# Moving the weight buffers of a split-precision transformer kernel to four different byte offsets from their matmul operands

## Chip, cores and metric

One Trainium2 chip, one NeuronCore of it. The metric is the device time of one execution of the whole program in microseconds (us), on that core. Engines are named as in the profile: PE is TensorE's matmul, PEld its weight load, DVE is VectorE, ACT is ScalarE, SP is the engine that issues the DMAs.

## What is computed

Two transformer blocks on 512 tokens of width 1024, all in float32. The first block has two layers; each is a SwiGLU feed-forward, a hybrid mixer (sliding-window attention, a gated linear recurrence, a short convolution) and a second feed-forward. The second block has one layer with low-rank attention, gated linear attention and a convolutional feed-forward. Cut to what the time goes into, it is a long row of products of the tokens with weights:

```python
def swiglu(h, w_gu, w_down):
    gu = h @ w_gu
    g, u = jnp.split(gu, 2, axis=-1)
    return (jax.nn.silu(g) * u) @ w_down
...
for l in range(DEPTH):
    h = modulate(x, g_norm[l, 0], mod[:, 0], mod[:, 1])
    x = x + 0.5 * mod[:, 2][:, None, :] * swiglu(h, w_ffn1_gu[l], w_ffn1_down[l])
    h = modulate(x, g_norm[l, 1], mod[:, 3], mod[:, 4])
    x = x + mod[:, 5][:, None, :] * hybrid_mixer(h, w_in[l], w_out[l], ...)
    h = modulate(x, g_norm[l, 2], mod[:, 6], mod[:, 7])
    x = x + 0.5 * mod[:, 8][:, None, :] * swiglu(h, w_ffn2_gu[l], w_ffn2_down[l])
```

## The kernel before

**Products in three matmuls.** [...] A product of weights w and tokens x is then made of three matmuls that add up in one PSUM bank: low weights with high tokens, high weights with low tokens, high weights with high tokens. The method `mm` issues them (lines 500, 501 and 502), eight chunks of 128 rows one after another, so 24 matmuls for one unit of weights with 128 output channels. In a matmul the weights are the stationary operand (`lhsT`, 128 columns, loaded by a LDWEIGHTS of its own before each matmul), the tokens are the moving one (`rhs`, 512 or 256 columns).

**Where the operands lie.** The token parts lie in slots of 2048 bytes in each partition: 36 slots `r0` to `r35`, and in most phases eight extra ones in the tile `xr` (method `xtype`). The weights come by DMA into a ring of four buffers `raw` (4096 bytes in each partition, 1024 float32). For each unit `split_next` takes the next buffer of the pool `hip` (tile `whi`) and of the pool `lop` (tile `wlo`); each pool has `WB` = 4 buffers, handed out in turn, so a unit belongs to one of four rounds. The method `split` fills both: ACT copies `raw` to `whi` (line 507), DVE writes `raw` minus `whi` to `wlo` (line 508). There are 450 such units, nearly all of 1024 or 896 columns.

**Addresses.** Pools are laid out one behind the other. In the program before, each slot `r` starts at 128 bytes past a multiple of 512 in its partition, and so does `xr`, because of a pool `gap` of 384 bytes that nothing uses. All eight weight buffers start at 384 past a multiple of 512 (`whi` from byte 173440, `wlo` from byte 189824, in steps of 4096). A matmul takes a piece of 128 columns, 512 bytes, from a weight buffer. So in every matmul of line 500, 501 or 502 the distance from the moving operand to the weights is 256 bytes, modulo 512.

**Order.** The order of instructions on each engine follows from the order in which the program issues them and from waits on tiles; addresses have no part in it. TensorE's weight load of the next matmul stands right behind the start of the current one.

Of the kernel before, what the change touches and what calls it, by code (L numbers as in the profile page):

```python
# [9 lines left out]
F32 = mybir.dt.float32  # L10
F32R = mybir.dt.float32r
# [16 lines left out]
P = 128  # L28
# [173 lines left out]
class Arena:  # L202


    def __init__(self):
        self.tiles = []
        self.free = []
        self.cur = 0
# [133 lines left out]
class Prog:  # L342
# [4 lines left out]
    def __init__(self, es, tc, d, out):  # L347
        self.es, self.tc, self.d, self.out = es, tc, d, out
        nc = self.nc = tc.nc
        self.T, self.V, self.A = nc.tensor, nc.vector, nc.scalar  # L350

        def mk(n, b, **k):
            return es.enter_context(tc.tile_pool(name=n, bufs=b, **k))

        cp = self.cp = mk("cp", 1)
        self.rawp = mk("rawp", self.RAW)
        self.hip = mk("hip", self.WB)
        self.lop = mk("lop", self.WB)
        self.sm = mk("sm", 12)
        mk("gap", 1).tile([P, 96], F32, name="gap")  # L360
        self.banks = Banks(tc)
        self.park = mk("dp", 1, space=bass.MemoryType.DRAM).tile([KD, P, S], F32, name="park")
        self.logits = mk("dl", 1, space=bass.MemoryType.DRAM).tile([16, P, S], F32, name="logits")
        self.F = Arena()
        self.F.add(cp.tile([P, self.NF * 512], F32, name="farena"), self.NF * 2)
        self.R = Slots([cp.tile([P, S], F32R, name=f"r{i}")[:, :] for i in range(36)])
        self.RX = Slots()
        self.xpool = None
        self.vecs = cp.tile([P, d["vecs"].shape[1]], F32, name="vecs")
        self.cst = cp.tile([P, 3 * P], F32, name="cst")  # L370
        self.ident = self.cst[:, 0:P]
        self.maskf, self.maskb = self.cst[:, P:2 * P], self.cst[:, 2 * P:3 * P]
        self.ones = cp.tile([P, P], F32, name="ones")
        self.eps = cp.tile([P, 1], F32, name="eps")
        self.sinks = cp.tile([P, 16], F32, name="sinks")
        self.nsink = cp.tile([P, 16], F32, name="nsink")
        self.mod = [cp.tile([P, 72], F32, name=f"mod{l}") for l in range(2)]
        self.mod2 = cp.tile([P, 48], F32, name="mod2")
        self.modc = cp.tile([P, 16], F32, name="modc")
        self.crow = [None] * 3  # L380
        self.units = []
        self.ready = {}
        self.ld = self.sp = self.tk = self.rt = self.nsplit = 0
        self.bg = []
        self.users, self.loader = [], None
# [69 lines left out]
    def split_next(self):  # L455
        u = self.units[self.sp]
        if self.ld <= self.sp:
            self.load_next()
        kind, ap, key, raw = u
        n = ap.shape[-1]  # L460
        if kind == "w":
            h = self.hip.tile([P, 1024], F32R, name="whi", tag="whi")
            lo = self.lop.tile([P, 1024], F32R, name="wlo", tag="wlo")
            self.split(raw[:, :n], h[:, :n], lo[:, :n])
            self.ready[self.nsplit] = (key, h, lo)
            self.nsplit += 1
        else:
            self.mod_unit(key, raw)
            if self.sp < EARLY:
                raw.done()  # L470
        u[3] = None
        self.sp += 1
        ahead = self.RAW + (4 if self.sp < EARLY - 8 else 0)
        while self.ld < len(self.units) and self.ld < self.sp + ahead:
            self.load_next()
# [1572 lines left out]
```

## Time and profile before

| | |
|---|---|
| median of 3 runs | 2715.85 us (2713.94 to 2716.39) |
| the profiled execution, its own time | 2715.99 us |
| its span, first to last instruction | 2714.2 us |
| PE busy | 2679.2 us, 99% |
| PEld busy | 2250.4 us, 83% |
| DVE busy | 1668.5 us, 61% |
| ACT busy | 1024.1 us, 38% |
| DMA queue q1 | 353.64 MB, 40.3% of 16 engines |
| granted TensorE clock, mean | 0.994 |

The span is the stretch of the profiled execution between its first and last instruction; the execution's own time is 1.8 us longer. A busy share is a mean over the whole span. [...]

### The profile page before, as it was taken

The numbers are of one execution on the slowest core, as the hardware profiler recorded it, in microseconds if no ns is written. First come the engines' busy times: TensorE is split into PE (matmuls) and PEld (weight loads), VectorE is DVE, ScalarE is ACT, GpSimd is POOL, SyncE is SP. The second block draws the span as 40 slices with busy tenths as digits, with TensorE's granted clock in tenths as the row PEclk, the third lists the DMA queues.
The fourth block names the chain that finished last, engine by engine and source line by source line (L and its number), as shares of the span: only waits on it lengthen the run. The fifth ranks groups of instructions, "written<-read, shape, count | busy, mean of one in ns | idle before, by whom it ended". The sixth has DMA issues, their size and how long they took to land.

```text
span 2714.2 us, 34099 instructions
## 1 busy us (share of the span) xinstructions
PE 2679.2 (99%) x13586; PEld 2250.4 (83%) x13586; DVE 1668.5 (61%) x2854; ACT 1024.1 (38%) x1603; POOL 0.2 (0%) x4
## 2 busy tenths in 40 slices
PE   8999999999999999999999999999999999999998
PEld 7888897898888988889879888888788767988887
DVE  7554468664444744446866865474576665786666
ACT  3322237442222422223654232253444664432322
POOL 0000000000000000000000000000000000000000
PEclk8999999999999999999999999999999999999999
DMA  7544443344444444444423666423222104233332
GB/s 286 194 140 149 152 141 131 115 142 146 147 151 146 139 158 145 149 144 155 146 71 113 209 208 195 147 88 117 82 91 70 58 28 155 86 101 97 91 98 64
DMA packets 105887, 355.81 MB, mean 131 GB/s; under 512 B 11776, under 2 KB 14976, under 8 KB 105472
## 3 DMA queue, kind: packets, MB, share of 16 engines
q1 hardware_dynamic: 105728, 353.64, 40.3%
q8 instruction: 106, 1.74, 0.3%
q14 instruction: 53, 0.43, 0.1%
HBM read 345.21 MB, written 8.39 MB: 130 GB/s over the span
## 4 chain that ended last, share of the span: by engine, by line
PE 93%; DVE 3%; ACT 2%; issue 1%; DMA 0%; SPq 0%; DVEq 0%; ACTq 0%
PE pb L500 28%; PE pb L501 28%; PE pb L502 28%; PE pb L1775 1%; PE pd L1747 1%; ACT farena L401 1%; PE pd L1764 1%; PE pb L618 1%; PE pb L2024 1%; PE pb L1168 1%; PE pb L2027 0%; PE pb L2028 0%; PE pb L1642 0%; PE pb L1115 0%; PE pb L1152 0%
## 5 line engine op out<-in xcount | busy, mean ns | idle before, releaser
L500 PE MATMUL pb<-r,wlo 128*128 128x512 f32 (+1 forms) x3360 | 1236.4, 369 | 1.2 <-DVE wlo L508 1.1
L501 PE MATMUL pb<-r,whi 128*128 128x512 f32 (+1 forms) x3360 | 1229.2, 367 | 0.0
L502 PE MATMUL pb<-r,whi 128*128 128x512 f32 (+1 forms) x3360 | 1229.1, 366 | 0.0
L507 ACT ACTIVATE whi<-raw 128x1024 fp32r<-128x1024 f32 (+2 forms) x450 | 465.0, 1034 | 807.5 <-issue 441.7
L500 PEld LDWEIGHTS pb<-r,wlo 128*128 128x128 f32 x3360 | 633.4, 189 | 113.3 <-issue 7.3
L502 PEld LDWEIGHTS pb<-r,whi 128*128 128x128 f32 x3360 | 634.1, 189 | 103.2 <-issue 0.2
L501 PEld LDWEIGHTS pb<-r,whi 128*128 128x128 f32 x3360 | 634.1, 189 | 102.3 <-issue 1.9
L508 DVE TENSOR_TENSOR wlo<-raw,whi 128x1024 fp32r<-128x1024 f32 (+2 forms) x450 | 535.9, 1191 | 207.9 <-ACT whi L507 207.0
L512 DVE CUSTOM_DVE_ANT_0 raw<-raw,farena 128x1024 f32<-128x1024 f32 x176 | 215.2, 1224 | 204.1 <-DMA raw<-wmod 144.3
L677 DVE SCALAR_TENSOR_TENSOR farena<-pb,mod,farena 128x512 f32<-128x512 f32 (+1 forms) x176 | 114.9, 653 | 203.8 <-PE pb L502 203.4
L500 PE MATMUL pb<-xr,wlo 128*128 128x512 f32 (+1 forms) x520 | 186.3, 358 | 0.0
L501 PE MATMUL pb<-xr,whi 128*128 128x512 f32 (+1 forms) x520 | 185.4, 356 | 0.0
L502 PE MATMUL pb<-xr,whi 128*128 128x512 f32 (+1 forms) x520 | 185.3, 356 | 0.0
L401 ACT ACTIVATE farena<-pb 128x512 f32<-128x512 f32 x93 | 55.6, 598 | 329.5 <-PE pb L502 325.5
L768 DVE TENSOR_TENSOR farena<-pb,farena 128x512 f32<-128x512 f32 x110 | 75.9, 691 | 158.9 <-PE pb L502 141.8
L820 DVE SCALAR_TENSOR_TENSOR farena<-pb,vecs,farena 128x441 f32<-128x441 f32 (+2 forms) x176 | 120.7, 693 | 42.7 <-ACT farena L812 39.4
L500 PEld LDWEIGHTS pb<-xr,wlo 128*128 128x128 f32 x520 | 98.2, 189 | 14.4 <-ACT xr L507 0.2
L501 PEld LDWEIGHTS pb<-xr,whi 128*128 128x128 f32 x520 | 98.3, 189 | 14.4 <-DVE xr L508 0.2
L502 PEld LDWEIGHTS pb<-xr,whi 128*128 128x128 f32 x520 | 98.2, 189 | 14.1
L574 ACT ACTIVATE farena<-farena 128x256 f32<-128x256 f32 (+1 forms) x97 | 44.9, 468 | 84.7 <-DVE farena L677 84.7
L401 ACT ACTIVATE farena<-farena 128x512 f32<-128x512 f32 (+2 forms) x89 | 51.3, 605 | 64.5 <-DVE farena L820 47.7
L645 ACT ACTIVATE r<-farena,mod 128x256 fp32r<-128x256 f32 (+1 forms) x119 | 55.4, 516 | 51.1 <-DVE farena L643 50.6
(275 smaller groups left out, 1843.9 us busy)
## 6 DMA issues: line engine op xcount, KB each, us to landing
raw<-gu SPq DMA_DIRECT2D x213, 512.0 KB, 3.6
raw<-wmod SPq DMA_DIRECT2D x128, 512.0 KB, 3.5
raw<-dn SPq DMA_DIRECT2D x80, 448.0 KB, 3.4
raw<-wada SPq DMA_DIRECT2D x48, 512.0 KB, 3.5
raw<-dn SPq DMA_DIRECT2D x40, 512.0 KB, 3.8
raw<-w2a SPq DMA_DIRECT2D x34, 512.0 KB, 3.5
raw<-win SPq DMA_DIRECT2D x32, 512.0 KB, 3.5
raw<-wout SPq DMA_DIRECT2D x24, 512.0 KB, 3.5
```

Of the source, the lines that this page charges most:

```text
L401: i = self.A.activation(out, in_, func, **k).ins
L500: self.T.matmul(acc, lhsT=lo[:, s], rhs=xh[:, tok], start=i == 0, stop=False)
L501: self.T.matmul(acc, lhsT=h[:, s], rhs=xl[:, tok], start=False, stop=False)
L502: self.T.matmul(acc, lhsT=h[:, s], rhs=xh[:, tok], start=False, stop=i == n - 1)
L507: self.A.activation(hi, src, AF.Copy)
L508: self.V.tensor_tensor(lo, src, hi.bitcast(F32), op=SUB)
L512: self.V.tensor_tensor_reduce(out=out, in0=raw, in1=row, scale=1.0, scalar=0.0, op0=MUL, op1=ADD, accum_out=col)
L574: self.A.activation(t[:, :n], src, AF.Square, scale=scale)
L645: self.A.activation(hi[:, tok], t[:, :n], AF.Identity, bias=sh[:, k:k + 1])
L677: self.V.scalar_tensor_tensor(x, acc[:, :n], gate[:, d:d + 1], x, op0=MUL, op1=ADD)
L768: self.V.tensor_tensor(a[:, :], acc[:, :], g[:, :], op=MUL)
L820: self.V.scalar_tensor_tensor(o, g[:, r0 + i - 1:r1 + i - 1, c0 + j - 1:c1 + j - 1], self.v(f"cw{i}{j}", f), o, op0=MUL, op1=ADD)
```

## The change

It adds two unused tiles of 256 bytes, cuts the one behind the small tiles from 384 to 128 bytes, and makes the weight buffers 1040 columns wide instead of 1024, of which the last 16 are never touched.

```diff
         self.rawp = mk("rawp", self.RAW)
+        mk("gap0", 1).tile([P, 64], F32, name="gap0")
         self.hip = mk("hip", self.WB)
+        mk("gap1", 1).tile([P, 64], F32, name="gap1")
         self.lop = mk("lop", self.WB)
         self.sm = mk("sm", 12)
-        mk("gap", 1).tile([P, 96], F32, name="gap")
+        mk("gap2", 1).tile([P, 32], F32, name="gap2")
...
-            h = self.hip.tile([P, 1024], F32R, name="whi", tag="whi")
-            lo = self.lop.tile([P, 1024], F32R, name="wlo", tag="wlo")
+            h = self.hip.tile([P, 1040], F32R, name="whi", tag="whi")
+            lo = self.lop.tile([P, 1040], F32R, name="wlo", tag="wlo")
```

A buffer is now 4160 bytes, 64 more than a multiple of 512, so the four rounds start at different places. What the built programs hold (bytes past a multiple of 512, in each partition; the distance is weights minus moving operand, modulo 512):

| | before | changed |
|---|---|---|
| slots r | 128 | 128 |
| whi and wlo, rounds 1 to 4 | 384, 384, 384, 384 | 128, 192, 256, 320 |
| extra slots xr | 128 | 384 |
| distance to r, rounds 1 to 4 | 256 in all | 0, 64, 128, 192 |
| distance to xr, rounds 1 to 4 | 256 in all | 256, 320, 384, 448 |

In a unit the high and the low part stand at the same distance. The order of instructions on every engine is the same in both programs, row for row, with the same waits; only line numbers and addresses differ.

## Rows read from the trace of the kernel before

**Rows 1.** The page, part 1: busy time and share of the span by engine

```profile
PE 2679.2 (99%) x13586; PEld 2250.4 (83%) x13586; DVE 1668.5 (61%) x2854; ACT 1024.1 (38%) x1603; POOL 0.2 (0%) x4
```

**Rows 2.** The page, part 4: the chain that ended last, by engine and by line

```profile
PE 93%; DVE 3%; ACT 2%; issue 1%; DMA 0%; SPq 0%; DVEq 0%; ACTq 0%
PE pb L500 28%; PE pb L501 28%; PE pb L502 28%; PE pb L1775 1%; PE pd L1747 1%; ACT farena L401 1%; PE pd L1764 1%; PE pb L618 1%; PE pb L2024 1%; PE pb L1168 1%; PE pb L2027 0%; PE pb L2028 0%; PE pb L1642 0%; PE pb L1115 0%; PE pb L1152 0%
```

**Rows 3.** The page, part 5, line 500 with slots r and xr: count, busy us, mean ns

```profile
L500 PE MATMUL pb<-r,wlo 128*128 128x512 f32 (+1 forms) x3360 | 1236.4, 369 | 1.2 <-DVE wlo L508 1.1
...
L500 PE MATMUL pb<-xr,wlo 128*128 128x512 f32 (+1 forms) x520 | 186.3, 358 | 0.0
```

**Rows 4.** Timeline of PE, 512 columns, feed-forward (start us, duration us, what): steps 0 and 24

```profile
1000.03 0.39 PE L502 MATMUL pb<-r,whi 128*128 128x512 f32 x1
...
1005.47 0.39 PE L502 MATMUL pb<-r,whi 128*128 128x512 f32 x1
```

**Rows 5.** Timeline of PEld, the weight load beside the matmul at 1000.03

```profile
1000.03 0.19 PEld L500 LDWEIGHTS pb<-r,wlo 128*128 128x128 f32 x1
```

**Rows 6.** Timeline of PE, 256 columns, slots r and xr mixed: steps 0 and 24

```profile
367.08 0.28 PE L501 MATMUL pb<-r,whi 128*128 128x256 f32 x1
...
369.96 0.28 PE L501 MATMUL pb<-r,whi 128*128 128x256 f32 x1
```

**Rows 7.** Timeline of PE at half clock: steps 0 and 3

```profile
450.61 0.63 PE L502 MATMUL pb<-r,whi 128*128 128x512 f32 x1
...
451.89 0.63 PE L502 MATMUL pb<-r,whi 128*128 128x512 f32 x1
```

**Rows 8.** Windows, full and half clock: stretch, busy by engine, PEclk, DMA share, GB/s

```profile
441.00:442.00 1.00, 1.00 (x6) 0.84 (x5) 0.97 (x2) 0.97 (x2) 0.00 (x0) 1.00 0.79 270
450.60:452.20 1.60, 1.60 (x5) 1.30 (x4) 1.59 (x9) 0.00 (x0) 0.00 (x0) 0.50 0.21 36
```

**Rows 9.** Timeline of PE, attention scores, distance 0: two pairs of 512 and 256 columns

```profile
2150.93 0.39 PE L1747 MATMUL pd<-xr,r 128*128 128x512 f32 x1
2151.16 0.28 PE L1748 MATMUL pd<-xr,r 128*128 128x256 f32 x1
...
2151.62 0.40 PE L1747 MATMUL pd<-xr,r 128*128 128x512 f32 x1
```

**Rows 10.** Timeline of PE after a stretch of other matmuls (line 1046): steps 0 to 3 and 8

```profile
428.20 0.40 PE L501 MATMUL pb<-r,whi 128*128 128x512 f32 x1
428.43 0.40 PE L502 MATMUL pb<-r,whi 128*128 128x512 f32 x1
428.66 0.40 PE L500 MATMUL pb<-r,wlo 128*128 128x512 f32 x1
428.90 0.39 PE L501 MATMUL pb<-r,whi 128*128 128x512 f32 x1
...
430.05 0.39 PE L500 MATMUL pb<-r,wlo 128*128 128x512 f32 x1
```

**Rows 11.** Lines by form, the two halves of the split: count, busy us, mean ns

```profile
L507 ACT ACTIVATE whi<-raw 128x1024 fp32r<-128x1024 f32 x356 | 376.7, 1059 | 604.4 <-issue 315.2 <-PE pb L502 260.5 <-PE pb L1433 20.3
L508 DVE TENSOR_TENSOR wlo<-raw,whi 128x1024 fp32r<-128x1024 f32 x356 | 434.8, 1222 | 172.7 <-ACT whi L507 171.9
```

**Rows 12.** The tile wlo: who waited for it (us, times)

```profile
  PEld pb L500: 1.3, 1
  PE pb L500: 1.1, 1
```

## The prediction

> **What bounds the kernel now.** I read the page from the top. The busy line says that PE works 99% of the span while DVE and ACT stand at 61% and 38% [rows 1]; the chain that ended last is PE for 93%, and 84% of it lies on the three lines 500, 501 and 502, in equal parts [rows 2]. So the time is the number of matmuls on these lines times the step from one start to the next, and the other engines matter only where PE waits for them. The count is 3360 with slots `r` and 520 with `xr` on line 500 [rows 3]; lines 501 and 502 have the same, which makes 3 x 3880 = 11640 matmuls. Some 400 more at the program's start and in the second block also use `whi` or `wlo`; I leave them out of the sum.
>
> The reader should not take the step from a matmul's duration, since matmuls overlap. In the timeline of a feed-forward 24 steps run from 1000.03 to 1005.47 us [rows 4], which is 5.44 us / 24 = 226.7 ns. [...] While a matmul runs, the weights of the next are being loaded; the load's row starts in the same hundredth of a microsecond [rows 4, 5]. [...]
>
> **The change part by part.** *Instructions.* None is added, removed or moved, on any engine or DMA queue, and the waits are the same. Cost 0.
>
> *The splits.* ACT and DVE still write 1024 columns for most units, at 1059 and 1222 ns [rows 11], to addresses that are shifted by multiples of 64 bytes. No row shows another offset, so I bound the effect by the cover: in the whole span PE waited 1.1 us, once, for `wlo`, and the weight load 1.3 us, once [rows 12], while DVE was idle for 39% of the span [rows 1]. A split slower by a tenth would add 0.12 us to each of 450 units, 55 us of DVE work beside some 1046 us that it has free; without that cover it would cost these 55 us. A faster one gives nothing. Cost 0.
>
> *The padding.* 64 unused bytes per buffer and three gaps; nothing reads them. Cost 0.
>
> *The distances.* This is the whole question. Before, all 11640 matmuls run at distance 256 modulo 512. Afterwards each round has a quarter of them, 2910: with slots `r` at 0, 64, 128 and 192, with `xr` at 256, 320, 384 and 448. The trace of before has no matmul at a distance of 64, 128 or 192, so its nearest rows must bound them:
>
> - Distance 0 is there: in the attention scores (lines 1747 and 1748) keys in `xr` stream past queries in `r`, both 128 bytes past a multiple of 512. Two pairs of 512 and 256 columns take 2151.62 - 2150.93 = 0.69 us, 345 ns a pair [rows 9]. At distance 256 such a pair is 226.7 + 120.0 = 346.7 ns [rows 4, 6]. That is the same within the 10 ns to which the rows are printed. So the round at 0 costs nothing.
> - Between buffers of one kind the addresses differ by multiples of 512, and `r` and `xr` lie in different parts of the memory. In the stretch of 256 columns both kinds alternate and the steps stay at 120.0 ns [rows 6]. So the upper address bits do nothing either.
> [...]
> - Upwards, the slowest step of such matmuls in these rows is 0.24 us, from 428.66 to 428.90 [rows 10], 13.3 ns over the settled one: 3 x 2910 x 13.3 ns = 116 us more.
>
> I take **0** for the three unseen distances, because the two that the trace does show, as far apart as the modulus 512 allows, agree, and so do `r` and `xr`. This is the nearest evidence, but it is evidence for two of eight places.
>
> [...]
>
> The sum: the profiled execution's own 2715.99 us + 0, which is 0.1 us off the median of the three runs, 2715.85 us. Forecast **2716 us**, with a range of its own of 2711 to 2721. Of this kernel a measurement can tell about 0.2%, 5.4 us, from no change.
>
> **The rivals.** *The rhythm is lost (slower).* The 226.7 ns are a rhythm into which the matmuls settle. After other work the steps wander: 8 steps from 428.20 to 430.05 us take 1.85 us, 231.3 ns each, with single steps of 230 and 240 ns [rows 10], before they settle. [...] The place is lines 500 to 502. If every unit, now at another distance than the one before, has to settle again, the price is 8 x (231.3 - 226.7) = 37 ns for 450 units: 17 us, 2733 us. If the steps never settle at the three new distances, it is 8730 x 4.6 ns = 40 us: **2756 us**. The bound is 2832 us, where each step takes 240 ns. [...] For it speaks the wandering itself; against it that distance 0 and distance 256, and a change from one to the other, cost the same.
>
> [...]
>
> *The change does not do what it says.* Then all rounds would stand at one distance. The addresses of the built program exclude this; and its time would be 2716 us too, so it gets no chance of its own.
>
> **How the numbers follow.** The forecast, no effect, gets 0.42: the seen distances agree, but six of eight are unseen. Slower gets 0.38: when a distance matters at all, mixing four of them in turn gives the rhythm three ways to be worse and a switch at each unit. Faster gets 0.20: it needs a freed round that is not given back by the others. These are also the chances of slower by over 0.2%, of within 0.2% and of faster by over 0.2%. For the range, the lower end is one freed round, 2677 us; more than one freed round, some 0.08, is left out. The upper end is half of the upper bound, 58 us: 2774 us, which holds both prices of the lost rhythm; the worse half, some 0.12, is left out.
>
> **What would show it.** In the timeline of the changed kernel the steps of lines 500 to 502 must be read unit by unit: in four units in a row, 24 steps each. All at 226.7 ns means that the forecast and its reason hold. [...] The pairs of lines 1747 and 1748, whose keys move from distance 0 to 256, should stay at 345 ns. The splits should stay near 1059 and 1222 ns, and PE's waits for `wlo` near 1 us. I am wrong if any round's step differs by over 1 ns from 226.7, since 2910 matmuls then already make 3 us; and wrong in the reasoning, though not in the time, if rounds differ and cancel.

## The result, and the profile after

The changed kernel takes 2742.62 us (median of four runs, 2740.77 to 2743.15). Beside it the kernel before took 2715.18 us (four runs, 2713.94 to 2716.39). The ratio is 1.010, with a 95% interval from 1.0082 to 1.0117: **slower by 1.0%**, inside the range of the prediction but not its forecast. The profiled execution took 2743.13 us with a span of 2741.4 us; the span before was 2714.2 us. Both have a mean granted clock of 0.994, so the 27.2 us between the spans are not the clock's.

The page of the changed kernel: busy time by engine, the chain by engine, and the groups that answer to [rows 3] (lines stand two lower, so 500 is now 502).

```profile
PE 2707.4 (99%) x13586; PEld 2247.0 (82%) x13586; DVE 1669.3 (61%) x2854; ACT 1022.4 (37%) x1603; POOL 0.2 (0%) x4
...
PE 93%; DVE 4%; ACT 2%; issue 1%; DMA 0%; SPq 0%; DVEq 0%; ACTq 0%
...
L502 PE MATMUL pb<-r,wlo 128*128 128x512 f32 (+1 forms) x3360 | 1245.0, 372 | 1.4 <-DVE wlo L510 1.2
...
L502 PE MATMUL pb<-xr,wlo 128*128 128x512 f32 (+1 forms) x520 | 187.0, 360 | 0.0
```

The counts are those of before, to the instruction. PE is busy 28.2 us longer (2707.4 against 2679.2) [rows 1], the others are as long as before to within 4 us. The chain is PE's for 93%, as it was [rows 2]. So the same matmuls are slower, and no new wait appears. Two views confirm the second half. The splits, by form, against [rows 11]:

```profile
L509 ACT ACTIVATE whi<-raw 128x1024 fp32r<-128x1024 f32 x356 | 376.1, 1057 | 625.8 <-issue 324.3 <-PE pb L504 273.1 <-PE pb L1435 20.7
...
L510 DVE TENSOR_TENSOR wlo<-raw,whi 128x1024 fp32r<-128x1024 f32 x356 | 434.5, 1221 | 192.7 <-ACT whi L509 192.2
```

And who waited for the tile `wlo`, against [rows 12]:

```profile
  PEld pb L502: 1.4, 1
  PE pb L502: 1.2, 1
```

Splits of 1057 and 1221 ns, and one wait of 1.2 us: nothing has changed here. What has changed is the step from one start to the next. The timeline of PE shows four units of a feed-forward in a row, at distances 128, 64, 0 and 192; of each unit the first and the last start of a run of steps stand here, of the second also the three behind the first.

```profile
1001.67 0.40 PE L503 MATMUL pb<-r,whi 128*128 128x512 f32 x1
...
1006.55 0.40 PE L503 MATMUL pb<-r,whi 128*128 128x512 f32 x1
...
1007.02 0.39 PE L502 MATMUL pb<-r,wlo 128*128 128x512 f32 x1
1007.25 0.40 PE L503 MATMUL pb<-r,whi 128*128 128x512 f32 x1
1007.49 0.39 PE L504 MATMUL pb<-r,whi 128*128 128x512 f32 x1
1007.72 0.40 PE L502 MATMUL pb<-r,wlo 128*128 128x512 f32 x1
...
1012.15 0.39 PE L503 MATMUL pb<-r,whi 128*128 128x512 f32 x1
...
1013.31 0.39 PE L502 MATMUL pb<-r,wlo 128*128 128x512 f32 x1
...
1018.07 0.39 PE L502 MATMUL pb<-r,wlo 128*128 128x512 f32 x1
1018.30 0.39 PE L503 MATMUL pb<-r,whi 128*128 128x512 f32 x1
1018.53 0.39 PE L504 MATMUL pb<-r,whi 128*128 128x512 f32 x1
...
1023.11 0.39 PE L503 MATMUL pb<-r,whi 128*128 128x512 f32 x1
```

- Distance 128: 21 steps in 4.88 us, 232.4 ns each.
- Distance 64: 22 steps in 5.13 us, 233.2 ns. Single steps alternate, 0.23 and 0.24 us.
- Distance 0: 21 steps in 4.76 us, 226.7 ns. This is the step of before [rows 4]. The stretch begins behind the unit's first three steps, which still take 229 to 232 ns.
- Distance 192: 20 steps from 1018.53, in 4.58 us, 229.0 ns.

The granted clock from 1000 to 1024 us is 1.00 in both kernels.

With 256 columns the same view shows the opposite. Here a unit at distances 0 and 256 ends, and one at 192 and 448 begins at 382.89:

```profile
380.73 0.28 PE L502 MATMUL pb<-r,wlo 128*128 128x256 f32 x1
...
382.89 0.28 PE L502 MATMUL pb<-xr,wlo 128*128 128x256 f32 x1
...
385.16 0.28 PE L504 MATMUL pb<-xr,whi 128*128 128x256 f32 x1
```

18 steps in 2.16 us are 120.0 ns, as in [rows 6]; the 20 steps that follow take 2.27 us, 113.5 ns. At half clock there is no such difference. Five steps at distance 128, and the window with its PEclk of 0.50:

```profile
456.56 0.63 PE L504 MATMUL pb<-r,whi 128*128 128x512 f32 x1
...
458.69 0.63 PE L503 MATMUL pb<-r,whi 128*128 128x512 f32 x1
```

```profile
456.60:458.60 2.00, 2.00 (x6) 1.61 (x5) 1.95 (x11) 0.00 (x0) 0.00 (x0) 0.50 0.29 96
```

2.13 us / 5 = 426 ns, as in [rows 7], whose clock is 0.50 as well [rows 8].

The score pairs of the attention, whose keys have moved from distance 0 to 256, against [rows 9]; the last row is the first matmul behind two pairs:

```profile
2176.76 0.39 PE L1749 MATMUL pd<-xr,r 128*128 128x512 f32 x1
...
2177.46 0.40 PE L503 MATMUL pb<-r,whi 128*128 128x512 f32 x1
```

Two pairs take 0.70 us, before 0.69.

**Where the 27 us are.** For each matmul with a weight piece as stationary operand the step up to its start can be read from the timeline and sorted by the distance that the built program gives it, here modulo 256. Means in ns; left out are steps over 153 ns for 256 columns or 287 ns for 512, which hold a wait or run at half clock, and the few short ones, up to 29 ns for 256 columns and 202 ns for 512 (together 2% of the steps, as many after as before):

| distance | before: 0 | after: 0 | 64 | 128 | 192 |
|---|---|---|---|---|---|
| 512 columns | 227.00 | 227.98 | 233.27 | 232.66 | 229.08 |
| such matmuls | 9084 | 2313 | 2271 | 2241 | 2259 |
| 256 columns | 119.83 | 119.64 | 115.73 | 118.54 | 116.34 |
| such matmuls | 2760 | 678 | 702 | 690 | 690 |

Number times difference: 2313 x 0.98 + 2271 x 6.27 + 2241 x 5.66 + 2259 x 2.08 ns = +33.9 us, and 678 x -0.19 + 702 x -4.10 + 690 x -1.29 + 690 x -3.49 ns = -6.3 us. Together +27.6 us, against 27.2 us between the spans: within the accuracy of such a sum the steps of these lines are the whole difference.

### The profile page after: what moved, and what is told of

Read it like the earlier page. It is cut to its first block, busy times and chain, and to the rows that moved or that the text cites. A ratio compares the mean times of both kernels' runs of the same rounds, so it can differ in the third digit from the quotient of the medians.

```text
span 2741.4 us, 34099 instructions
## 1 busy us (share of the span) xinstructions
PE 2707.4 (99%) x13586; PEld 2247.0 (82%) x13586; DVE 1669.3 (61%) x2854; ACT 1022.4 (37%) x1603; POOL 0.2 (0%) x4
## 4 chain that ended last, share of the span: by engine, by line
PE 93%; DVE 4%; ACT 2%; issue 1%; DMA 0%; SPq 0%; DVEq 0%; ACTq 0%
PE pb L502 28%; PE pb L503 28%; PE pb L504 28%; PE pb L1777 1%; ACT farena L403 1%; PE pd L1749 1%; PE pd L1766 1%; PE pb L620 1%; PE pb L1170 1%; DVE wlo L510 0%; PE pb L1644 0%; PE pb L1117 0%; PE pb L1154 0%; PE pb L1433 0%; PE pb L1435 0%
## 5 line engine op out<-in xcount | busy, mean ns | idle before, releaser
L510 DVE TENSOR_TENSOR wlo<-raw,whi 128x1024 fp32r<-128x1024 f32 (+2 forms) x450 | 535.4, 1190 | 230.7 <-ACT whi L509 230.0
L576 ACT ACTIVATE farena<-farena 128x256 f32<-128x256 f32 (+1 forms) x97 | 44.8, 467 | 83.6 <-DVE farena L679 83.6
```

Source lines behind the costliest of these rows:

```text
L510: self.V.tensor_tensor(lo, src, hi.bitcast(F32), op=SUB)
L576: self.A.activation(t[:, :n], src, AF.Square, scale=scale)
```

## Experiments

Each changes the kernel before, but for e8. In e1 to e7 and e9 the weight buffers are 1088 columns wide (4352 bytes), and the piece in use begins `o` columns in, so that `o` sets the distance in steps of 4 bytes:

```diff
-            h = self.hip.tile([P, 1024], F32R, name="whi", tag="whi")
-            lo = self.lop.tile([P, 1024], F32R, name="wlo", tag="wlo")
-            self.split(raw[:, :n], h[:, :n], lo[:, :n])
+            o = 0
+            h = self.hip.tile([P, 1088], F32R, name="whi", tag="whi")[:, o:o + n]
+            lo = self.lop.tile([P, 1088], F32R, name="wlo", tag="wlo")[:, o:o + n]
+            self.split(raw[:, :n], h, lo)
```

**One distance for all (e1, e2, e9).** e1 is this diff: wider buffers, rounds at 256 and 0 in turn. e2 has `o = 16` (distance 64), e9 has `o = 4` (distance 16), each modulo 256.

> Weight buffers 4352 bytes long instead of 4096, so that the four rounds stand at distances 256 and 0 modulo 512 in turn; no 64, 128 or 192. Theory A (the distance modulo 256 sets the step of a matmul, and 0 and 256 are the same place): 2715 us, as before, with 226.7 ns per 512 columns and 120 ns per 256. Rival B (changing the distance from unit to unit disturbs the rhythm, whatever the distances are): slower, up to the 2742 us of the change. Rival C (longer buffers or moved small tiles cost by themselves): 2742 us.

> As e1, but every unit is written 64 bytes into its buffer, so that all matmuls with weights run at distance 64 modulo 256 and none changes. Theory A: the steps that the changed kernel shows in its round at 64, 233.3 ns per 512 columns and 115.7 ns per 256, now in all: 9084 x 6.3 ns - 2760 x 4.1 ns = +57 - 11 us, 2761 us. Rival B (the mixing costs): no switches, so 2715 us.

> All units 16 bytes into their buffers, so every product runs at distance 16. In the scan by 16 bytes a unit at 16 came after one at 0 and took 227 to 228 ns per 512 columns; in the scan by 4 bytes it came after one at 12 and took 233 ns. If a distance has two rhythms and the matmuls before decide which is taken, this kernel shows both in turn, or one of them throughout: 9084 x 0 to 6.3 ns, 2713 to 2772 us. If the distance alone decides, all its steps are 227 to 228 ns and it takes 2715 to 2724 us.

Measured: e1 2715.14 us, ratio 1.0002 [0.9993, 1.0011], steps 227.02 and 119.82 ns. Padding, another pitch and a change between 256 and 0 at each unit cost nothing. e2 2758.04 us, 1.0164 [1.015, 1.0178], steps 233.34 and 115.18 ns: by the sum above 9084 x 6.34 - 2760 x 4.65 ns = +44.8 us, and 42.9 us came. So the cost comes with the distance itself, with no mixing of distances. e9 2763.94 us, 1.0178 [1.0163, 1.0193], the slowest of all, 233.02 and 118.37 ns. The timeline of PE of e2:

```profile
1000.27 0.40 PE L501 MATMUL pb<-r,wlo 128*128 128x512 f32 x1
...
1005.87 0.40 PE L501 MATMUL pb<-r,wlo 128*128 128x512 f32 x1
```

And of e9, two stretches:

```profile
441.06 0.39 PE L503 MATMUL pb<-r,whi 128*128 128x512 f32 x1
...
446.50 0.39 PE L503 MATMUL pb<-r,whi 128*128 128x512 f32 x1
...
1000.17 0.40 PE L502 MATMUL pb<-r,whi 128*128 128x512 f32 x1
...
1005.77 0.40 PE L502 MATMUL pb<-r,whi 128*128 128x512 f32 x1
```

At 1000 us each kernel has 24 steps in 5.60 us, 233.3 ns: these are not steps that wander for a while and settle, but a lasting pace. The stretch of e9 at 441 us has 24 steps in 5.44 us, 226.7 ns, at the same distance of 16 and at full clock (at half clock 24 steps would take 10.2 us, at 426 to 427 ns each). So this distance has two lasting rhythms, as the first of the two cases in the expectation had it.

The traces show when one is taken: where a stream of matmuls begins. Call a stream a row of matmuls of one width that no longer step interrupts. e9 has 17 streams of 512 columns with 35 steps or more. Behind their first few steps 13 of them run at 233 ns to their end, one over 1487 steps, and 4 at 227 ns; none changes on the way. In the kernel before, at distance 0, all 20 such streams come down to 227 ns within some ten steps and stay there. In e2, at distance 64, all 17 stay at 233 ns.

**Which operand's place (e10, e11, e8).** e10 moves slots and weights by 64 bytes together; e11 moves the slots by 64 bytes and leaves the weights where they were, both modulo 256; e8 is the changed kernel with the extra slots `xr` put back to the place that `r` has, modulo 512.

```diff
 e10 and e11, ahead of the slots:
+        cp.tile([P, 16], F32, name="pada")
 e11 also, behind them:
+        cp.tile([P, 48], F32, name="padb")
-        mk("gap", 1).tile([P, 96], F32, name="gap")
+        mk("gap", 1).tile([P, 112], F32, name="gap")
 e8, against the changed kernel:
-        mk("gap2", 1).tile([P, 32], F32, name="gap2")
+        mk("gap2", 1).tile([P, 96], F32, name="gap2")
```

> The kernel before with 64 unused bytes ahead of the slots: slots and weight buffers all move by 64, the distance stays 256. Theory A (the distance between the two counts): 2715 us, 226.7 ns per 512 columns. Rival E (the place of the weights by themselves counts: 128 bytes past a multiple of 256 is the good one, now it is 192): the steps that the change shows one place further on, 233.3 ns, 2758 us.

> The kernel before with the slots r and xr moved by 64 bytes and the weight buffers by 256: the weights stay at 128 past a multiple of 256, the distance becomes 192 modulo 256. Theory A: the changed kernel's steps at 192 in all matmuls, 9084 x 2.2 ns - 2760 x 3.9 ns = +20 - 11 us, 2724 us. Rival E: 2715 us.

> The change with one part undone: the unused tile behind the small tiles is 384 bytes again, so that the extra slots xr stand like the slots r and all products run at 0, 64, 128 and 192 in turn. Theory A (distance modulo 256): the 256 bytes do nothing, 2742 us as with the change. Rival (the 1560 matmuls with xr suffer from distances over 256): 1560 x 5 ns = 8 us less at most, 2734 us.

Measured: e10 2713.9 us, 0.9998 [0.9989, 1.0007]; e11 2726.07 us, 1.0044 [1.0031, 1.0056]. PE's timeline of e10:

```profile
1000.22 0.39 PE L503 MATMUL pb<-r,whi 128*128 128x512 f32 x1
...
1005.66 0.39 PE L503 MATMUL pb<-r,whi 128*128 128x512 f32 x1
```

And of e11:

```profile
1000.01 0.39 PE L503 MATMUL pb<-r,whi 128*128 128x512 f32 x1
...
1005.51 0.39 PE L503 MATMUL pb<-r,whi 128*128 128x512 f32 x1
```

24 steps of 226.7 ns in e10, of 229.2 ns in e11. The place of the weights is the same modulo 256 in e11 and before; only the distance to the slots is another, 192, and its step is that of the round at 192 in the changed kernel (229.08). In e10 the slots have moved as in e11, and the weights with them, and nothing changes; so neither operand's place by itself counts. The **distance between the two operands** sets the pace. e8 2742.78 us, 1.0099 [1.0082, 1.0116], every mean within 0.1 ns of the changed kernel's: the 256 bytes that the extra slots were moved do nothing. With e1 this says that distances count modulo 256.

**Finer distances (e4, e7).** e4 steps through 0, 16, ... 240 bytes from unit to unit (`o = 4 * (self.nsplit % 16)`), e7 through 0, 4, ... 60 (`o = self.nsplit % 16`).

> Sixteen distances in turn, unit by unit: 0, 16, 32 to 240 bytes, each for 28 units. Read is the step per distance and per number of columns, not the time. Theory A: each distance has its own step, with 226.7, 233, 232.7 and 229 ns at 0, 64, 128 and 192 for 512 columns, and 120, 116, 118.5 and 116 for 256; between them some distance may be better than 0 for 512 columns. Rival D (only the place within 64 bytes is without effect): 16, 32 and 48 have the same steps as 0.

> Sixteen distances in steps of 4 bytes: 0, 4 to 60. If lines of 16 bytes are what load and stream share, the steps change at 16, 32 and 48 and not within them, apart from pieces that begin inside such a line and touch one line more; 0 stays at 227 ns, 16 at 228, 32 and 48 at 233. If the distance itself counts, they change smoothly with 4, 8 and 12.

Measured, one run each: 2751.32 and 2755.96 us. Mean steps of 512 columns in ns:

| e4, distance | 0 | 16 | 32 | 48 | 64 | 80 | 96 | 112 | 128 | 144 | 160 | 176 | 192 | 208 | 224 | 240 |
|---|---|---|---|---|---|---|---|---|---|---|---|---|---|---|---|---|
| | 227.6 | 228.4 | 233.1 | 233.3 | 233.3 | 231.8 | 234.0 | 233.3 | 233.4 | 233.4 | 233.4 | 230.0 | 230.0 | 233.1 | 233.6 | 228.2 |

| e7, distance | 0 | 4 | 8 | 12 | 16 | 20 | 24 | 28 | 32 | 36 | 40 | 44 | 48 | 52 | 56 | 60 |
|---|---|---|---|---|---|---|---|---|---|---|---|---|---|---|---|---|
| | 227.8 | 232.5 | 230.7 | 231.1 | 233.3 | 232.7 | 231.1 | 234.7 | 233.1 | 234.2 | 233.3 | 230.4 | 233.3 | 233.4 | 233.3 | 230.7 |

With 512 columns no distance lies below 0, and already 4 bytes make a difference: the steps change within 16 bytes, and not smoothly, so neither case of the expectation of e7 holds. Distance 16 reads 228.4 ns in e4, where it follows a unit at 0, and 233.3 ns in e7, where it follows one at 12: a matmul's step also hangs on those before it. Both scans go through the distances in one order only, so a column of these tables stands for a distance behind its neighbour, and e2, e9 and e11 are the cleaner readings. With 256 columns e4 gives 113.9 ns at 64 as the lowest, 119.5 ns at 0.

**High and low part apart (e5, e6).** e5 leaves the high part (`whi`) at 0 and moves the low one (`wlo`) as e4 does; against e1:

```diff
             o = 0
+            q = 4 * (self.nsplit % 16)
...
-            lo = self.lop.tile([P, 1088], F32R, name="wlo", tag="wlo")[:, o:o + n]
+            lo = self.lop.tile([P, 1088], F32R, name="wlo", tag="wlo")[:, q:q + n]
```

e6 is the other way round, with `o = 4 * (self.nsplit % 16)` and `q = 0`.

> High parts at distance 0 in all units, low parts at 0, 16, 32 to 240 in turn. Of three matmuls in a row, only the one of line 502 runs while low weights are being loaded; the one of line 500 uses low weights. Theory A1 (the load that runs beside the stream sets the step): the step of line 502's matmul varies with the distance, up to 233 ns and more, and lines 500 and 501 come back towards 227 ns. Theory A2 (the weights in use set it): line 500 varies and lines 501 and 502 stay. If the rhythm carries over from matmul to matmul, all three vary.

> The reverse: low parts at distance 0, high parts at 0, 16 to 240 in turn. Theory A1: lines 500 and 501 vary with the distance and line 502 comes back towards 227 ns. A combination of distances whose mean step is below 226.7 ns per 512 columns would give a kernel faster than before; theory A expects none by over 1 ns.

Measured, one run each: 2747.2 and 2744.72 us. It was meant to tell whether the weights in use or those being loaded count, by which of the three lines gets slow. It didn't: in e5 each of the three gets slow somewhere, and not the same ones each time. From a matmul's start to the next one's, on what were lines 500, 501 and 502 before, the means are 228.5, 232.8 and 238.6 ns with the low part at 32; 234.4, 228.3 and 228.7 at 64; 227.7, 227.5 and 227.5 at 144. This fits the third case of the expectation, a rhythm that carries over from matmul to matmul; how it does so isn't shown. In e6 the means run from 227.3 (at 16) to 233.1 ns (at 128). No pair of distances gives less than the 226.7 ns of 0 and 0.

**Distance by width (e3).** Units whose matmuls have 256 columns go to distance 64, the others stay at 0. The function `narrow` names them by their keys:

```diff
+            o = 16 if narrow(key) else 0
```

> As e1 with distance 0, but the units that are multiplied with half of the tokens at a time (256 columns) are written 64 bytes into their buffers: 2568 matmuls of 256 columns at distance 64, all 9084 of 512 columns at 0. Theory A: 2568 x 4.1 ns = 10.5 us less than before, 2704 to 2705 us. Rival B: the distance changes some 80 times between groups of units, so 2715 us or a few us more.

Measured: 2707.48 us (2706.31 to 2708.86), ratio 0.9976 [0.9967, 0.9985]. This **beats both kernels**, the one before by 0.24%. By the trace 2568 matmuls of 256 columns go from 119.83 to 116.21 ns, which is 9.3 us, of which 7.7 us came between the medians; those of 512 columns stay at 227.02 ns. Of the 10.5 us that were expected, 1.2 us are missing because the mean step is not as short as the 4.1 ns of the changed kernel said: at 64 there are two rhythms, and the mean hangs on how many matmuls run in each. The other 1.6 us are not accounted for; the interval reaches from 4 to 9 us. PE's timeline of e3, two stretches of 24 steps:

```profile
528.74 0.28 PE L512 MATMUL pb<-r,wlo 128*128 128x256 f32 x1
...
531.56 0.28 PE L512 MATMUL pb<-r,wlo 128*128 128x256 f32 x1
...
562.07 0.28 PE L514 MATMUL pb<-r,whi 128*128 128x256 f32 x1
...
564.79 0.28 PE L514 MATMUL pb<-r,whi 128*128 128x256 f32 x1
```

117.5 ns in the first, 113.3 ns in the second. The first stands mostly at 64 and the second mostly at 320, but both go from a unit at the one to a unit at the other without a change of pace, and the means at the two are within 1 ns of each other. As in e9, the rhythm belongs to the stream: of 31 streams of 256 columns in e2 21 run at 113 ns and 10 at 118, and none changes on the way; in e3 17 and 14. Which of the two a stream falls into at its start wasn't found.

## Why the prediction was wrong, step by step

The time, 2742.6 us, lies inside the range of 2677 to 2774, because the range was drawn around the rivals; the forecast of no effect, and the reason for it, were wrong.

- *Instructions, splits, padding: 0 each.* Right: the same counts, splits of 1057 and 1221 ns, one wait of 1.2 us, and e1, which has 256 bytes of padding in each buffer and distances of 0 and 256 alone, came out at 1.0002.
- *"The round at 0 costs nothing", "the upper address bits do nothing".* Right. After a switch the steps need a few matmuls (227.98 ns as a mean instead of 227.00), 2.3 us in the whole program. The score pairs of the attention, now at 256, stay within what their printed starts can tell: two pairs take 0.70 us, before 0.69 [rows 9].
- *"I take **0** for the three unseen distances, because the two that the trace does show, as far apart as the modulus 512 allows, agree".* **This step failed**, the term of 0 for three rounds. e1 and e8 show that the distance counts modulo 256. So 0 and 256 are the same place, and their agreement was evidence for one place of four, not for two of eight. The three others cost 6.27, 5.66 and 2.08 ns a matmul at 512 columns. The test that the prediction set, one round's step over 1 ns from 226.7, came out against it in three rounds.
- *One price for the 2910 matmuls of a round, whatever their width.* At 64 the matmuls of 512 columns take 233.27 ns against 227.00 at 0 before, those of 256 columns 115.73 against 119.83: one width loses 6.27 ns and the other gains 4.10. That is why the sum had one line where it needed two.
- *The rival "the rhythm is lost".* Its strong form comes nearest to what happened: at the three new distances the steps don't settle at 226.7 ns, in the place that it named. It was priced at 8730 x 4.6 = 40 us. The mean of the three rounds is +4.7 ns, but on 6771 matmuls of 512 columns (31.6 us); the 2082 of 256 columns gave 6.2 us back. That 4.7 is so near 4.6 is luck: the 4.6 was read where a stream restarts at distance 256 [rows 10], and 4.7 is a mean of 6.27, 5.66 and 2.08. Its mild form was priced at 17 us for 450 units; it came only in the quarter that returns to 0, and 2.3 us were measured. Its word for what happens was off too: at 64 and 16 the steps do not wander but keep a steady mean of 233.3 ns over 24 steps (e2, e9).
- *"... the lower end is one freed round, 2677 us".* This term, 39 us less on 2910 matmuls, 13.4 ns each, no run shows. For 512 columns none of the distances of e4 and e7 goes below 227.6 ns. For 256 columns there are shorter steps than at 0, 113.3 ns at best (e3) against 120.0 [rows 6], and e3 turns them into 7.7 us.
- *Whether a step of 64 bytes makes a difference.* It does; so do 4 bytes, with 227.8 ns at 0 and 232.5 at 4 (e7).

With the same instructions, a shift of the slots against the weights by 64 bytes takes a matmul of 512 columns from 226.7 to 229.2 ns (e11), and a shift of both leaves it at 226.7 (e10): at full clock what a matmul takes hangs on where its two operands lie against each other. At half clock the distance makes no difference: 512 columns take 426 to 427 ns at 0, 16, 64, 128 and 192 alike (the kernel before, e9, e2, the changed kernel, e11). Whether PE waits at full clock for a read of the memory or for something of its own, no run shows.

**What stays open.** What in the chip makes the distance count, why its period is 256 bytes (e1, e8), and why 512 columns run best at 0 and 256 columns at 64, the runs don't say. They leave open as well whether the weights in use or those being loaded count, since e5 and e6 couldn't part the two, and which rhythm a stream falls into where there are two: it is settled where the stream begins, but what settles it wasn't found.

## What to carry to other kernels

In this kernel a chain of matmuls with a load each sets the time, and the distance between stationary and moving operand is a parameter of it: 0 was best for 512 columns and 64 for 256 (227.6 and 113.9 ns in e4), and the runs spread from 2707.48 us (e3) to 2763.94 us (e9), 2.1%, with nothing else changed. What it is worth elsewhere, no run here shows. To find out, read the step, not the duration, for each width by itself, and scan the distance once, over the 256 bytes after which it repeated here (e1, e8), each time with one distance in the whole kernel, since a scan unit by unit mixes a distance with the one before it (at 16 bytes 228.4 ns in e4 and 233.3 in e7). And before two equal observations are counted as two, ask whether they may be the same point of a period.

## What the runs showed that was not expected

- Distances act modulo 256 bytes (227.02 ns with 0 and 256 in turn in e1, 227.00 before) and differ from 4 bytes on: 227.8 ns at 0, 232.5 ns at 4 (e7).
- The order is reversed by width: at 64, +6.3 ns for 512 columns and -4.1 ns for 256 in the changed kernel.
- One distance has two lasting rhythms: 113.3 and 117.5 ns at 64 with 256 columns (e3), 226.7 and 233.3 ns at 16 with 512 (e9). A stream keeps the one that it has after its first steps.
- At distance 0 the slow rhythm doesn't last: in the kernel before all 20 streams of 512 columns come down to 227 ns within some ten steps.
- Steps repeat in short patterns: in the four units shown of the changed kernel, 231 and 236 ns in turn at distance 64, and 229, 232 and 226 ns at 192.
